# A two-layer diffusion block on one core: the second product of the first FFN by Strassen's scheme, and modulations of layer 1 in other stages

## The chip, the core and the metric

The kernel runs on one core of a Trainium2 chip. The core has a matrix engine (TensorE, PE in the profile; its weight loads are PEld), three engines for elementwise work (VectorE is DVE, ScalarE is ACT, GpSimd is POOL), and SP, whose queue issues most DMAs. TensorE reads SBUF and accumulates in PSUM; VectorE and ScalarE read both memories; GpSimd reads SBUF only. The metric is the device time of one execution in microseconds.

## The reference, cut to what matters

Two layers are applied to 256 tokens `x` and 256 context tokens `ctx`, both of width 1024. Each layer modulates the normalized input, mixes tokens, and runs a convolutional FFN of hidden width 2816. In layer 0 both sequences go through all of it; in layer 1 the context goes into the mixer only.

```python
m = (jax.nn.silu(c) @ mod_w[layer] + mod_b[layer])       # six vectors of 1024, mc likewise from c_ctx
sh1, sc1, g1, sh2, sc2, g2 = jnp.split(m, 6, axis=-1)    # called parts 0 to 5 below
def conv_ffn(u, w_up, conv_w, conv_b, w_down):
    a = dwconv3(u @ w_up, conv_w, conv_b)                # 1024 -> 5632, three taps along the tokens
    gate, val = jnp.split(a, 2, axis=-1)
    return (jax.nn.silu(gate) * val) @ w_down            # 2816 -> 1024: the "second product"
x = x + g2 * conv_ffn(modulate(x, norm2_g, sh2, sc2), ...)
xc = xc + g2c * conv_ffn(modulate(xc, norm2_g, sh2c, sc2c), ...)     # layer 0 only
```

All is float32.

## The kernel before, in words

**Products.** Each float32 operand is split into a high part in the fp32r format, made by ScalarE (`split_w`, L185), and the remainder, made by VectorE as a subtraction with both operands in SBUF (L186). One product of two split operands is a triple of matmuls (`mm3`, L191 to L193): high x high, high x low, low x high. Weights come by DMA on SP's queue in "raw" tiles of 1 MB (`load_raw`), two or more of which exist; the split pieces of 1024 columns have four buffers each for high and low.

**First FFN** (`ffn` with layer 0, called in `layer0`). The hidden width is 22 blocks of 128, taken in pairs, in two parts of 12 and 10 blocks. For every block there are a gate and a value product of 8 triples over 512 columns (256 `x` tokens and 256 context tokens) into one PSUM bank each. `conv3` evacuates a bank: one ScalarE instruction (L459) and two VectorE taps that read PSUM (L462, L463). ScalarE applies silu (L519), GpSimd multiplies gate and value (L520), ScalarE and VectorE split the result into `gh` and `gl` (L521, L522). At the end of a part, for each of two column halves and four token tiles of 128, the second product runs over the part's blocks (`gemm_b`); `resid` multiplies the bank with the gate row `G` and adds it to `x`, both on VectorE (L444, L446). In the last part ScalarE sums the squares for the next norm.

**Modulations.** The layer-0 gate of the FFN and all six parts of layer 1 are computed inside this stage, between pairs and column halves, as "fillers" (`fl`). A filler is one call of `mod_vec` for half a part: four loads of 512 KB (two 128-row slices of weights each), and for each of one or two sequences one multiplication (L306) and seven multiply-accumulates (L308) of 128x512 on VectorE, four TensorE transposes (L312), and a reduction (L314) with one or two small instructions behind it. `gate_rows` makes the rows of `G` from the layer-0 gate: GpSimd builds eight diagonal matrices (L333), TensorE multiplies them with ones.

**Layer 1.** `norm_mod` normalizes both sequences; then the GLA stage (`gla_proj`, `gla_chain`, `gla_out`) interleaves projections with chains of small products on all engines; an output projection, and the second FFN (`ffn` with layer 1) on the 256 `x` tokens. `gate_cols` (L344) spreads a gate over the partitions with TensorE; for the second FFN's gate it stands in the written-out order before that FFN.

**Order.** The tile framework gives each engine its list, in an order that it plans with costs of its own; each engine works through its list in order. Inside `manual_schedule` blocks the order of the named engines is the program's. SP's queue is in order too: a load that waits for its buffer holds up the loads behind it.

Of the kernel before, what the change touches and what calls it, by code (L numbers as in the profile page):

```python
# [9 lines left out]
F32 = mybir.dt.float32  # L10
# [7 lines left out]
D = 1024  # L18
# [88 lines left out]
class Kern:  # L107
# [52 lines left out]
    def load_raw(self, W, kb0, nkb, c0, n):  # L160

        pool, bufs = self.wp, self.RB
        if self.rawp:
            self.nraw += 1
            if self.nraw % (self.RB + self.rawp[1]) >= self.RB:
                pool, bufs = self.rawp
        raw = pool.tile([128, 2048], F32, tag="raw", bufs=bufs, name="raw")
# [7 lines left out]
    def split_w(self, v, pool=None):  # L175
# [11 lines left out]
        return hv, lv  # L187

# [40 lines left out]
    def setup(self):  # L229
        nc, A, const = self.nc, self.A, self.const  # L230
        ncol = sum(k for _, k in COLS)

# [60 lines left out]
    def mod_vec(self, layer, part, half, seqs):  # L293
# [4 lines left out]
        acc = [self.modp.tile([128, 512], F32, tag="macc", bufs=2, name="macc") for s in seqs]  # L298
        for h in range(4):
            raw = self.modp.tile([128, 2, 512], F32, tag="mraw", bufs=self.MB, name="mraw")  # L300
            nc.sync.dma_start(out=raw, in_=W[h * 256 : h * 256 + 256, c0 : c0 + 512].rearrange("(k p) n -> p k n", p=128))
            for k in range(2):
                for s in seqs:
                    c, w = self.cs[:, 2 * h + k, s : s + 1], raw[:, k, :]
# [52 lines left out]
    def square(self, pool, ss, t, c):  # L357

        sq = pool.tile([128, 512], F32, tag="sq", bufs=2, name="sq")
        act = self.nc.scalar.activation(sq, self.x[:, t, c * 512 : c * 512 + 512], AF.Square, accum_out=ss[:, c : c + 1])  # L360
        self.sq_act = act.ins

    def normed(self, pool, ss, t, inplace=False, act=0):
        nc = self.nc
        s1 = pool.tile([128, 1], F32, tag="s1", bufs=4, name="s1")
        nc.gpsimd.tensor_tensor(s1, ss[:, 0:1], ss[:, 1:2], op=ALU.add)
        r = self.rstd(pool, s1, 1, D, "rs")
# [111 lines left out]
    def ffn(self, pool, gpool, layer, nseq, G, fillers, sss, first=None, behind=(), ahead={}):  # L479
# [9 lines left out]
        for p0, p1 in parts:  # L489
# [37 lines left out]
            for c in range(2):  # L527
                self.gemm_b(gt, list(range(p1 - p0)), tiles, Wd, p0, c * 512, 512, mkres(c),
                            last=2 if (c == 1 and p1 == NHB) else 1)
                if fillers:  # L530
                    fillers.pop(0)()

# [304 lines left out]
    def layer0(self):  # L837
# [134 lines left out]
        with fb:  # L972

            with self.pool("ffn0") as fp, self.pool("ffn0g") as fg:
                self.modp, self.MB = fp, 4
                G = fg.tile([128, 2, D], F32, name="G2")
                self.rawp, self.nraw = (fg, 1), -1
# [5 lines left out]
                fl += [lambda p=p, h=h: self.mod_vec(1, p, h, (0, 1) if p < 2 else (0,)) for p in range(6) for h in range(2)]  # L983
# [3 lines left out]
                self.ffn(fp, fg, 0, 2, G, fl, self.sss, first, s0)  # L987
# [194 lines left out]
    def gla_out(self, pool, hp, att, X, Q, K, S=None, later=False):  # L1182
# [14 lines left out]
        os_ = pool.tile([128, 4, 128], F32, tag="gos", bufs=1, name="gos")  # L1197
# [18 lines left out]
    def layer1(self, g4):  # L1216
        nc, A = self.nc, self.A
        W = A["hg_w_in"][0]
        with ExitStack() as bk:
            bk.enter_context(self.banks("hg", mm=4, ga=2, tp=2))  # L1220
            with self.pool("n3") as np_:
                self.norm_mod(np_, self.sss, (0, 1), 1, 0)
            with self.pool("hg") as hg:
# [47 lines left out]
                with self.pool("gla") as gp:  # L1271
                    pr = self.gla_proj(gp, 0, ((), (), self.anch[0], self.anch[1]))
                    ch = self.gla_chain(gp, *pr)
                    values(0)
                    pr = self.gla_proj(gp, 1)
                    self.gla_out(gp, 0, *ch)
                    ch = self.gla_chain(gp, *pr)
                    pr = self.gla_proj(gp, 2)
                    self.gla_out(gp, 1, *ch)
                    ch2 = self.gla_chain(gp, *pr)  # L1280
                    pr = self.gla_proj(gp, 3)
# [10 lines left out]
                    with self.tc.manual_schedule(engines={mybir.EngineType.PE}):  # L1292

                        part_out(acc, w, [(0, 0), (0, 2), (0, 1), (1, 0), (0, 3), (1, 2)])
                        self.gla_turn(3, o3)
                        part_out(acc, w, [(1, 1), (1, 3)])
                        part_out(acc, w, [(k, j) for k in (2, 3) for j in (0, 2, 1, 3)])
                with self.pool("hgo") as hgo:
# [9 lines left out]
                    with self.tc.manual_schedule(engines={E.PE, E.DVE, E.Activation}):  # L1308
# [26 lines left out]
                        self.gate_cols(G4, 1, 5, (0,))  # L1335
# [17 lines left out]
                        self.gate_cols(G4, 1, 5, (1,))  # L1353
# [67 lines left out]
```

## Time and profile before

| | us |
|---|---|
| median of 3 runs | 1172.29 (1170.65 to 1175.51) |
| profiled execution | 1175.04 |
| its span, first to last instruction | 1173.3 |
| TensorE busy | 1137.6 (97%) |
| VectorE busy | 861.5 (73%) |
| ScalarE busy | 519.7 (44%) |
| GpSimd busy | 276.2 (24%) |

The profile is one execution. An engine is busy while an instruction runs on it. Ends of matmuls are modelled and overlap their neighbours, so the distance from start to start is the better price of one. VectorE's instructions also overlap by a little, so that sums of lengths over a stretch are larger than the busy time of the stretch. Idle time is put down to the event that ended it.

### The profile page before, as it was taken

The page shows a single profiled execution, that of the slowest core. Times are in us where ns is not written, and L with a number is a line of the kernel's source. Part 1 is how long each engine was busy: PE and PEld are TensorE (multiplying, and loading weights), DVE is VectorE, ACT ScalarE, POOL GpSimd, SP SyncE. Part 2 cuts the span into 40 slices and gives each one's busy share as a digit, 9 for nine tenths or more (in the row PEclk, how much of TensorE's full clock was granted, in tenths as well). Part 3 has the DMA queues.
Part 4 walks back from the last instruction along what each step waited for, and adds up shares of the span by engine and source line. Part 5 has one row for each costly group of instructions (what it writes and reads, how often), then busy time and mean ns, then how long its engine had stood idle before and what let it go on. Part 6 is the DMA issues. An engine that isn't in the chain of part 4 may idle for free. (4 is left out here: it accounts for less than half of the span.)

```text
span 1173.3 us, 17955 instructions
## 1 busy us (share of the span) xinstructions
PE 1137.6 (97%) x7094; PEld 928.2 (79%) x7094; DVE 861.5 (73%) x1284; ACT 519.7 (44%) x896; POOL 276.2 (24%) x285
## 2 busy tenths in 40 slices
PE   7999988999999999999999999999999999999997
PEld 3587865445888888888888888888888989999985
DVE  4668897786669997989988447565767766877753
ACT  3554333433245444212444236445465456666542
POOL 3110333341011142100111001535657311111110
PEclk9999999998999999999999999999999999999999
DMA  9543221454135552657764223323223354565550
GB/s 338 189 126 90 81 73 43 148 175 154 64 128 196 181 177 93 207 203 246 257 203 138 90 73 108 108 80 102 73 77 105 109 179 140 183 199 173 171 195 36
DMA packets 118055, 167.57 MB, mean 143 GB/s; under 512 B 4658, under 2 KB 74866, under 8 KB 117908
## 3 DMA queue, kind: packets, MB, share of 16 engines
q1 hardware_dynamic: 117540, 165.38, 42.7%
q8 instruction: 56, 0.92, 0.3%
q10 hardware_dynamic: 432, 1.05, 0.2%
q14 instruction: 27, 0.22, 0.1%
HBM read 165.37 MB, written 1.05 MB: 142 GB/s over the span
## 5 line engine op out<-in xcount | busy, mean ns | idle before, releaser
L186 DVE TENSOR_TENSOR lo<-raw,hi 128x1024 fp32r<-128x1024 f32 (+1 forms) x205 | 262.0, 1282 | 151.0 <-ACT hi L185 146.7
L185 ACT CAST hi<-raw 128x1024 fp32r<-128x1024 f32 (+1 forms) x205 | 213.5, 1047 | 325.0 <-PE mm L192 191.8
L192 PE MATMUL mm<-al,hi 128*128 128x512 f32 (+2 forms) x992 | 340.2, 344 | 1.2 <-DVE al L420 1.0
L191 PE MATMUL mm<-ah,hi 128*128 128x512 f32 (+2 forms) x992 | 339.9, 345 | 1.0 <-DVE ah L419 1.0
L193 PE MATMUL mm<-ah,lo 128*128 128x512 f32 (+2 forms) x992 | 340.1, 344 | 0.0
L192 PEld LDWEIGHTS mm<-al,hi 128*128 128x128 f32 x992 | 188.1, 190 | 23.2 <-DVE al L420 1.5
L191 PEld LDWEIGHTS mm<-ah,hi 128*128 128x128 f32 x992 | 187.5, 190 | 23.8 <-DVE ah L419 1.4
L193 PEld LDWEIGHTS mm<-ah,lo 128*128 128x128 f32 x992 | 188.0, 190 | 22.1 <-issue 0.5
L520 POOL TENSOR_TENSOR y<-y 128x512 f32<-128x512 f32 (+1 forms) x44 | 53.5, 1216 | 377.2 <-DVE y L463 319.4
L308 DVE SCALAR_TENSOR_TENSOR macc<-mraw,cs,macc 128x512 f32<-128x512 f32 x140 | 111.1, 804 | 8.7 <-DMA mraw<-in_mod_w_dram 8.0
L191 PE MATMUL mm<-hi,gh 128*128 128x512 f32 x242 | 94.6, 391 | 0.0
L193 PE MATMUL mm<-hi,gl 128*128 128x512 f32 x242 | 94.3, 390 | 0.0
L192 PE MATMUL mm<-lo,gh 128*128 128x512 f32 x242 | 94.2, 390 | 0.0
L191 PE MATMUL mm<-hi,ah 128*128 128x512 f32 (+1 forms) x192 | 74.7, 389 | 0.3 <-DVE modc L285 0.3
L192 PE MATMUL mm<-lo,ah 128*128 128x512 f32 (+1 forms) x192 | 73.7, 384 | 0.0
L193 PE MATMUL mm<-hi,al 128*128 128x512 f32 (+1 forms) x192 | 73.3, 385 | 0.0
L1159 POOL TENSOR_TENSOR gQ<-gQ,gT 128x256 f32<-128x256 f32 x56 | 54.7, 997 | 47.2 <-PE ga L1129 20.4
L1152 DVE TENSOR_TENSOR gK<-gK,gT 128x512 f32<-128x512 f32 (+1 forms) x56 | 50.6, 948 | 13.6 <-ACT gkc L1105 10.4
L193 PEld LDWEIGHTS mm<-hi,gl 128*128 128x128 f32 x242 | 45.4, 188 | 9.5
L192 PEld LDWEIGHTS mm<-lo,gh 128*128 128x128 f32 x242 | 45.4, 188 | 9.3
L191 PEld LDWEIGHTS mm<-hi,gh 128*128 128x128 f32 x242 | 45.4, 188 | 9.2
L459 ACT ACTIVATE y<-mm,col 128x512 f32<-128x512 f32 (+1 forms) x74 | 50.9, 687 | 2.6 <-DVE gl L522 2.6
(301 smaller groups left out, 1779.4 us busy)
## 6 DMA issues: line engine op xcount, KB each, us to landing
mraw<-in_mod_w_dram SPq DMA_DIRECT2D x96, 512.0 KB, 4.7
raw<-in_ffn_w_up_dram SPq DMA_DIRECT2D x44, 1024.0 KB, 5.6
raw<-in_ffn_w_down_dram SPq DMA_DIRECT2D x20, 1024.0 KB, 5.1
raw<-in_hg_w_in_dram SPq DMA_DIRECT2D x20, 1024.0 KB, 5.0
raw<-in_ab_w_in_dram SPq DMA_DIRECT2D x6, 1024.0 KB, 5.2
raw<-in_ab_w_out_dram SPq DMA_DIRECT2D x4, 1024.0 KB, 5.0
raw<-in_hg_w_out_dram SPq DMA_DIRECT2D x4, 1024.0 KB, 5.0
x<-in_x_dram SPq DMA_DIRECT2D x2, 1024.0 KB, 8.3
```

The source lines that it names most:

```text
L185: nc.scalar.copy(hv, v)
L186: nc.vector.tensor_tensor(lv, v, hv.bitcast(F32), op=ALU.subtract)
L191: mm(ps, lhsT=l[0], rhs=r[0], start=start, stop=False)
L192: mm(ps, lhsT=l[0], rhs=r[1], start=False, stop=False)
L193: return mm(ps, lhsT=l[1], rhs=r[0], start=False, stop=stop)
L308: nc.vector.scalar_tensor_tensor(acc[s], w, c, acc[s], op0=ALU.mult, op1=ALU.add)
L459: nc.scalar.activation(y, ps, AF.Identity, scale=w[1], bias=b)
L520: nc.gpsimd.tensor_tensor(ys[1], ys[0], ys[1], op=ALU.mult)
L1152: nc.vector.tensor_tensor(kv, kv, tv, op=ALU.mult)
L1159: nc.gpsimd.tensor_tensor(qv, qv, tq, op=ALU.mult)
```

## The change

The second product of the first FFN is done by a Strassen scheme. In each part the activations are a 2x2 block matrix: rows are the two sequences (`c` for context, `x`), columns the even and the odd blocks of the hidden width; the weights are the matching 2x2 of even and odd blocks by column halves. Seven products of quarters replace eight; they need sums of activation quarters and of weight quarters, which GpSimd makes in float32 before the split, and sums of products, which VectorE makes from one PSUM and one SBUF operand. The parts are now of 3, 3, 2 and 3 pairs. The residual multiplications and additions move to GpSimd, apart from some in the last part. Of layer 1's modulations, parts 3 and 4 (four calls) move into the GLA stage and part 5 (two calls) with its `gate_cols` into the second FFN; outside the first FFN a call loads eight tiles of 256 KB into four tiles kept from the first FFN. In every call ScalarE does the first multiplication. The context's last residual addition is made in layer 1, after the normalization of `x`.

```diff
     def mod_vec(self, layer, part, half, seqs):
+        own, nk = self.modp, 2 if self.modp else 1
+        if own:
+            acc = [own.tile([128, 512], F32, tag="macc", bufs=2, name="macc") for s in seqs]
+        else:
+            acc = [self.const.tile([128, 512], F32, tag="e4", bufs=1, name="macc")]
+        for h in range(8 // nk):
+            if own:
+                raw = own.tile([128, 2, 512], F32, tag="mraw", bufs=self.MB, name="mraw")
+            else:
+                raw = self.const.tile([128, 512], F32, tag=("e1", "u2")[h // 2 % 2], bufs=2, name="mraw").unsqueeze(1)
...
                     if h == 0 and k == 0:
-                        nc.vector.tensor_scalar(acc[s], w, c, None, op0=ALU.mult)
+                        nc.scalar.mul(acc[s], w, c)
...
+    def ffn_both(self, pool, gpool, G, fillers, sss, first, behind):
+        parts = [(0, 3), (3, 6), (6, 8), (8, 11)]
+        A11, A22, A12, S1, S2, S3, S4 = range(7)
+        gh = gpool.tile([128, 3, 7, 256], F32R, name="gh")
+        gl = gpool.tile([128, 3, 7, 256], F32R, name="gl")
...
+        for pa, pb in parts:
+            m, end = pb - pa, pb == 11
+            for pair in range(pa, pb):
...
+                if last:
+                    r11, r12, r22 = quarter(0, 0, pa, m), quarter(0, 1, pa, m), quarter(1, 1, pa, m)
...                                        # up products as before
+                        if last and b > b0:
+                            X = self.raw_tile()[:, : m * 512].rearrange("p (k n) -> p k n", k=m)
+                            nc.gpsimd.tensor_tensor(X, r22, r12, op=ALU.subtract)
+                            nc.gpsimd.tensor_tensor(r12, r12, r11, op=ALU.subtract)
+                            w11 = split(r11)
+                            nc.gpsimd.tensor_tensor(r11, X, r11, op=ALU.add)
+                            r21 = quarter(1, 0, pa, m)
...                                        # conv3, silu, GpSimd product y as before
+                        if b == b0:
+                            nc.scalar.copy(gh[:, g, A11, :], y[:, 256:])
+                            lower(gl[:, g, A11, :], gh[:, g, A11, :], y[:, 256:])
+                        else:
+                            P(sa[:, :256], x1, x2, op=ALU.add)
+                            P(sa[:, 256:], sa[:, :256], c1, op=ALU.subtract)
+                            both(sa, S1)
+                            both(y, A22)
+                            P(sb[:, :256], c1, x1, op=ALU.subtract)
+                            P(sb[:, 256:], c2, sa[:, 256:], op=ALU.subtract)
+                            both(sb, S3)
+                if fillers:
+                    fillers.pop(0)()
...
+            def add(dst, a, b, s=None, c=0, e=nc.vector if end else nc.gpsimd):
+                for t in range(2):
+                    nc.vector.tensor_tensor(dst[t], a[t], b[t], op=ALU.add)
+                    if s is not None:
+                        xs = self.x[:, 2 * s + t, c * 512 : c * 512 + 512]
+                        e.tensor_tensor(dst[t], dst[t], G[:, s, c * 512 : c * 512 + 512], op=ALU.mult)
+                        e.tensor_tensor(xs, xs, dst[t], op=ALU.add)
...
+            product(p1, A11, w11, alls)
+            for t in range(2):
+                nc.scalar.copy(e1[t], p1[t])
+            p6, w6 = banks(), split(r11)
+            nc.gpsimd.tensor_tensor(r11, r21, r11, op=ALU.subtract)
+            p2, w2 = banks(), split(r21)
+            product(p6, S2, w6, head)
+            product(p2, A12, w2, head)
+            product(p6, S2, w6, tail)
+            product(p2, A12, w2, tail)
+            add(u2, e1, p6)
+            add(e1, e1, p2, 1, 0, nc.gpsimd)
+            with self.tc.manual_schedule(engines={E.PE, E.DVE, E.Activation}) if end else ExitStack():
+                product(p5, S1, split(r12), alls)
+                w7 = split(X)
+                add(v, u2, p5)
+                product(p7, S3, w7, alls)
+                w4 = split(r11)
+                add(e4, v, p7, 0, 1, nc.gpsimd)
+                add(u2, u2, p7)
+                product(p4, A22, w4, alls)
+                w3 = split(r22)
+                add(u2, u2, p4, 0, 0)
+                product(p3, S4, w3, alls)
+            if end:
+                self.early = {t: self.factor(self.const, sss[t]) for t in range(2)}
+                add(v, v, p3)
+                for t in range(2):
+                    nc.vector.tensor_tensor(v[t], v[t], G[:, 1, 512:], op=ALU.mult)
+                self.to_ctx = v
+            else:
+                add(v, v, p3, 1, 1, nc.gpsimd)
...
-                self.modp, self.MB = fp, 4
+                self.modp, self.MB = fp, 2
-                self.rawp, self.nraw = (fg, 1), -1
+                self.rawp, self.nraw = (fg, 3), -1
-                fl += [lambda p=p, h=h: self.mod_vec(1, p, h, (0, 1) if p < 2 else (0,)) for p in range(6) for h in range(2)]
+                fl += [lambda p=p, h=h: self.mod_vec(1, p, h, (0, 1) if p < 2 else (0,)) for p in range(3) for h in range(2)]
-                self.ffn(fp, fg, 0, 2, G, fl, self.sss, first, s0)
+                self.ffn_both(fp, fg, G, fl, self.sss, first, s0)
...                                        # layer 1: four calls of mod() around the GLA steps
+                    mods = [(p, h) for p in (3, 4) for h in range(2)]
+                    def mod():
+                        with self.after(self.anch[1]):
+                            self.mod_vec(1, *mods.pop(0), (0,))
...                                        # second FFN
+                fl = [lambda h=h: self.mod_vec(1, 5, h, (0,)) for h in range(2)]
+                fl += [lambda h=h: self.gate_cols(G4, 1, 5, (h,)) for h in range(2)]
-                self.ffn(fp, fp, 1, 1, G4, [], sss, first, s0, ahead)
+                self.ffn(fp, fp, 1, 1, G4, fl, sss, first, s0, ahead)
```

## Rows read from the trace of the kernel before

**Rows 1.** The page: busy us, share of the span, instructions.
```profile
PE 1137.6 (97%) x7094; PEld 928.2 (79%) x7094; DVE 861.5 (73%) x1284; ACT 519.7 (44%) x896; POOL 276.2 (24%) x285
```

**Rows 2.** Stretches: length, busy us of PE, PEld, DVE, ACT, POOL; clock, DMA.
```profile
362.00:705.00 343.00, 343.00 (x1550) 283.33 (x1549) 285.16 (x396) 121.84 (x161) 50.20 (x36) 1.00 0.51 169
...
705.00:960.00 255.00, 254.46 (x2425) 218.99 (x2424) 171.32 (x209) 135.82 (x264) 115.10 (x119) 1.00 0.32 106
960.00:1120.00 160.00, 157.99 (x1233) 153.34 (x1232) 116.39 (x178) 96.87 (x165) 19.26 (x28) 1.00 0.51 169
```

**Rows 3.** Longest of PE's waits, 338 to 720 us: total us, times, longest.
```profile
PE tp L390 <- ACT hm L395: 0.8, 1, 0.8
```

**Rows 4.** Timeline, 676 to 745 us, PE: start, length, engine, line, operation.
```profile
676.07 0.39 PE L193 MATMUL mm<-hi,gl 128*128 128x512 f32 x1
...
678.79 0.39 PE L193 MATMUL mm<-hi,gl 128*128 128x512 f32 x1
...
681.74 0.60 PE L312 MATMUL sc<-ident,macc 128*128 128x128 f32 x4
...
682.09 0.48 PE L191 MATMUL mm<-hi,gh 128*128 128x512 f32 x1
```

**Rows 5.** Timeline of DVE, 386 to 404 us.
```profile
392.85 0.67 DVE L522 TENSOR_TENSOR gl<-y,gh 128x512 fp32r<-128x512 f32 x1
393.45 1.40 DVE L308 SCALAR_TENSOR_TENSOR macc<-mraw,cs,macc 128x512 f32<-128x512 f32 x2
...
396.10 1.21 DVE L186 TENSOR_TENSOR lo<-raw,hi 128x1024 fp32r<-128x1024 f32 x1
397.24 0.73 DVE L308 SCALAR_TENSOR_TENSOR macc<-mraw,cs,macc 128x512 f32<-128x512 f32 x1
397.90 0.73 DVE L462 SCALAR_TENSOR_TENSOR y<-mm,col,y 128x510 f32<-128x510 f32 x1
```

**Rows 6.** DVE's groups by form, 362 to 705 us: busy us, mean ns; idle before.
```profile
L308 DVE SCALAR_TENSOR_TENSOR macc<-mraw,cs,macc 128x512 f32<-128x512 f32 x132 | 105.6, 808 | 8.7 <-DMA mraw<-in_mod_w_dram 8.0
L186 DVE TENSOR_TENSOR lo<-raw,hi 128x1024 fp32r<-128x1024 f32 x61 | 78.5, 1287 | 33.2 <-ACT hi L185 32.8
...
L522 DVE TENSOR_TENSOR gl<-y,gh 128x512 fp32r<-128x512 f32 x22 | 16.5, 749 | 4.6 <-ACT gh L521 4.5
...
L446 DVE TENSOR_TENSOR x<-x,rtmp 128x512 f32<-128x512 f32 x14 | 9.5, 684 | 0.1
...
L306 DVE TENSOR_SCALAR macc<-mraw,cs 128x512 f32<-128x512 f32 x18 | 9.1, 506 | 0.0
```

**Rows 7.** POOL's groups by form, 362 to 705 us.
```profile
L520 POOL TENSOR_TENSOR y<-y 128x512 f32<-128x512 f32 x22 | 36.5, 1659 | 256.0 <-DVE y L463 221.2 <-ACT y L519 25.0 <-DVE modc L315 9.8
L333 POOL TENSOR_TENSOR gdg<-ident,ghi 128x512 fp32r<-128x512 f32 x4 | 6.0, 1506 | 10.1 <-DVE ghi L352 6.9 <-PE sc L334 3.1
```

**Rows 8.** Timeline of DVE and of POOL, 563 to 578 us.
```profile
564.46 2.31 DVE L186 TENSOR_TENSOR lo<-raw,hi 128x1024 fp32r<-128x1024 f32 x1
...
573.57 3.23 DVE L308 SCALAR_TENSOR_TENSOR macc<-mraw,cs,macc 128x512 f32<-128x512 f32 x3
...
564.05 1.64 POOL L520 TENSOR_TENSOR y<-y 128x512 f32<-128x512 f32 x1 [80.59 <-DVE y L463]
573.82 1.64 POOL L520 TENSOR_TENSOR y<-y 128x512 f32<-128x512 f32 x1 [8.14 <-DVE y L463]
```

**Rows 9.** Single lines of code (the last: tile gh): ns least/median/most.
```profile
L186 DVE TENSOR_TENSOR lo<-raw,hi x61: 1204/1218/2312, 362.3 to 694.4; 128x1024 fp32r<-128x1024 f32 x61
L308 DVE SCALAR_TENSOR_TENSOR macc<-mraw,cs,macc x132: 731/743/1772, 361.7 to 644.2; 128x512 f32<-128x512 f32 x132
L520 POOL TENSOR_TENSOR y<-y x22: 1288/1642/2780, 368.6 to 658.2; 128x512 f32<-128x512 f32 x22
L462 DVE SCALAR_TENSOR_TENSOR y<-mm,col,y x44: 729/739/746, 358.6 to 656.5; 128x510 f32<-128x510 f32 x44
L522 DVE TENSOR_TENSOR gl<-y,gh x44: 405/546/1776, 372.8 to 1111.4; 128x512 fp32r<-128x512 f32 x22, 128x256 fp32r<-128x256 f32 x22
```

More of the change, by code (lines that the diff above doesn't have):

```diff
@@ L160, in load_raw @@
     def load_raw(self, W, kb0, nkb, c0, n):
[L162 to L167, printed above, removed]
+        raw = self.raw_tile()
         v = raw[:, : nkb * n].rearrange("p (k n) -> p k n", k=nkb)
@@ L187, in split_w, with raw_tile @@
         return hv, lv
+    def raw_tile(self):
+        pool, bufs = self.wp, self.RB
+        if self.rawp:
+            self.nraw += 1
+            if self.nraw % (self.RB + self.rawp[1]) >= self.RB:
+                pool, bufs = self.rawp
+        return pool.tile([128, 2048], F32, tag="raw", bufs=bufs, name="raw")
     def mm3(self, ps, l, r, start, stop):
@@ L231, in setup @@
         ncol = sum(k for _, k in COLS)
+        for tag in ("e1", "e1", "u2", "u2", "v", "v", "e4"):
+            const.tile([128, 512], F32, tag=tag, bufs=1 if tag == "e4" else 2, name=tag)
         self.ones = const.tile([128, 128], F32R, name="ones")
@@ L297, in mod_vec @@
         W = self.A["mod_w"][layer]
[L298 to L302, printed above, removed]
+        own, nk = self.modp, 2 if self.modp else 1
[8 more added lines that the diff above has]
+                raw = self.const.tile([128, 512], F32, tag=("e1", "u2")[h // 2 % 2], bufs=2, name="mraw").unsqueeze(1)
+            rows = nk * 128
+            nc.sync.dma_start(out=raw, in_=W[h * rows : h * rows + rows, c0 : c0 + 512].rearrange("(k p) n -> p k n", p=128))
+            for k in range(nk):
                 for s in seqs:
-                    c, w = self.cs[:, 2 * h + k, s : s + 1], raw[:, k, :]
+                    c, w = self.cs[:, nk * h + k, s : s + 1], raw[:, k, :]
                     if h == 0 and k == 0:
-                        nc.vector.tensor_scalar(acc[s], w, c, None, op0=ALU.mult)
+                        nc.scalar.mul(acc[s], w, c)
                     else:
@@ L1221, in layer1 @@
             with self.pool("n3") as np_:
-                self.norm_mod(np_, self.sss, (0, 1), 1, 0)
+                self.norm_mod(np_, self.sss, (0,), 1, 0)
+                normed = self.xn_dve
+                with self.after(self.anch[0]):
+                    for t in (2, 3):
+                        xs = self.x[:, t, 512:]
+                        nc.vector.tensor_tensor(xs, xs, self.to_ctx[t - 2], op=ALU.add)
+                        self.square(np_, self.sss[t], t, 1)
+                self.norm_mod(np_, self.sss, (1,), 1, 0)
             with self.pool("hg") as hg:
@@ L1294, in layer1 @@
                         part_out(acc, w, [(0, 0), (0, 2), (0, 1), (1, 0), (0, 3), (1, 2)])
+                        part_out(acc, w, [(1, 1), (1, 3)])
+                        part_out(acc, w, [(2, j) for j in (0, 2, 1, 3)])
                         self.gla_turn(3, o3)
-                        part_out(acc, w, [(1, 1), (1, 3)])
-                        part_out(acc, w, [(k, j) for k in (2, 3) for j in (0, 2, 1, 3)])
+                        part_out(acc, w, [(3, j) for j in (0, 2, 1, 3)])
                 with self.pool("hgo") as hgo:
@@ L1386, in run @@
         self.anch = {}
+        self.early = {}
         self.ORDER = [("c1", 1, 0, 2), ("c1", 0, 0, 1), ("H", 0), ("hy", 2), ("c1", 0, 1, 1), ("H", 1), ("pv", 0, False), ("hy", 3),
```

111 lines of the change are left out of this document (101 added, 10 removed).

## The prediction

> **What bounds the kernel now.** I read the busy totals first: TensorE is busy 97% of the span, VectorE 73% [rows 1]. Then the stretches. The stage that the change rewrites, the first FFN, fills 362 to 705 us: there TensorE is busy 343.00 of 343 us, VectorE 285.16 (83%), ScalarE 121.84, GpSimd only 50.20; the two later stretches that receive the moved modulations hold VectorE at 171 of 255 us and 116 of 160 us, TensorE again nearly full [rows 2]. TensorE's waits from 338 to 720 us are three, the longest of 0.8 us [rows 3]. So the stage ends when TensorE has gone through its list, and a matmul that is taken away is worth its start-to-start distance, unless another engine fills its 343 us first. VectorE has 58 us to spare. The question is what the change puts there.
>
> **TensorE.** The second product is now 22 k-blocks x 4 token tiles x 2 column halves = 176 triples of matmuls. Seven products of quarters are 7 x 2 tiles x 11 k-blocks = 154 triples, of the same shape (128 weights columns, 512 moving). That removes 22 x 3 = 66 matmuls. From 676.07 to 678.79 us twelve such matmuls start, 0.227 us each [rows 4]; the busy time of one is longer because neighbours overlap. 66 x 0.227 = 15.0 us. Six modulation calls (parts 3, 4, 5) also leave the stage; each has four transposes, which push the next matmul back from 681.74 to 682.09 us [rows 4], so 6 x 0.35 = 2.1 us leave here and come back later. TensorE's floor in this stretch falls from 343 to 326 us.
>
> **VectorE, by its own work.** Its instructions start closer together than they last: 0.60 us for a 128x512 subtraction, 0.66 for a scalar_tensor_tensor, 1.14 for a 128x1024 subtraction [rows 5]. The edits at these distances:
> - Modulations: seven accumulating instructions for each call and sequence. 140 fall to 98: -42 x 0.66 = -27.7. The 20 first products go to ScalarE: 0.51 us long [rows 6], about 0.42 apart, -8.4. Six reductions less with their small followers: about -4.
> - Low parts of weights: 22 of 1024 columns (25.1 us) become, for each part of three pairs, 7 x (1.14 + 0.60) = 12.2, three times, and 8.0 for the part of two pairs: 44.5. +19.4.
> - Low parts of activations: 22 x 0.60 = 13.2 become, per pair, three of 512 columns and one of 256 (0.405 us long at least [rows 9], so about 0.34 apart), 11 x 2.14 = 23.5. +10.3.
> - Sums of products: 14 per part, 56 x 0.60 = +33.6.
> - Residual: 16 multiplications and 16 additions leave VectorE, -32 x 0.60 = -19.2; six come back in the last part, +3.6.
>
> Sum +8 us: 285 becomes 293 of 326 us. By this alone VectorE still fits, and the gain of TensorE would stand.
>
> **GpSimd, and what it does to VectorE.** In units of one 128x512 operation, GpSimd has 30 in this stage now: 22 gate-by-value products and 8 diagonal matrices for the gate rows [rows 7]. The change adds four combinations of weight quarters, 4 x 11 = 44 units; four sums of 256 columns per pair, 22; and the residual, 16 units in each of the first three parts and 8 in the last, 56. That makes 152 units.
>
> These are not free for VectorE. From 564.05 us GpSimd runs one product for 1.64 us; a subtraction that VectorE issues at 564.46 lasts 2.31 us in place of 1.22. From 573.82 the next one runs, and three accumulations last 3.23 us together; alone they would have taken 2 x 0.66 + 0.74 = 2.06 [rows 5, 8]. The same shows in the spread: the subtractions of 1024 columns have median 1.218 and maximum 2.312 us, the accumulations 0.743 and 1.772, the GpSimd product 1.288 at least and 2.780 at most, while the convolution taps, which read PSUM, stay between 0.729 and 0.746 [rows 9]. So a VectorE instruction with both operands in SBUF and a GpSimd operation hold each other up; one that reads PSUM is not touched.
>
> Price per unit: mean less median, times count, is (0.808 - 0.743) x 132 = 8.6, (1.287 - 1.218) x 61 = 4.2, and (0.749 - 0.68) x 22 = 1.5 us [rows 6, 9]; 0.68 is the undisturbed length of a 128x512 subtraction [rows 5, 6]. 14.3 us over 30 units is 0.48 us each. The bounds are far apart: zero, if every unit falls under a PSUM-reading instruction or an idle VectorE, and 1.1 to 1.2, what the two collisions of [rows 8] cost when VectorE had SBUF work queued. I take 0.48: it is a mean over the same instructions, at a VectorE load of 83%. About a third of VectorE's time afterwards is PSUM-reading work (88 taps x 0.66 + 56 sums x 0.60 = 92 us of 293), not very different from now, but long combinations of 1536 columns hide worse than short ones and a fuller VectorE hides less. So the value errs on the low side rather than the high one.
>
> 152 x 0.48 = 73 us, against 14.3 now: +59. VectorE 293 + 59 = 352 us, more than TensorE's 326. VectorE becomes the bound of the stage, in-order, with the weight splits that TensorE needs standing behind modulations and sums; the four buffers of split pieces are the slack between the two. With 3% idle left in VectorE the stage takes 352 / 0.97 = 363 us in place of 343: +20 us. ScalarE gets some 42 us more (casts, copies, first products at about the lengths of now) and stays near 164 of 363. What GpSimd itself has, 152 x 1.29 = 196 us plus waits, fits.
>
> In sentences of their own: the Trainium skill, page "SBUF — State Buffer", section "SBUF: two separate sides", calls this port pair an exclusive lock that the first comer keeps for its whole instruction, for a VectorE instruction with two SBUF inputs against a GpSimd one. The collisions above agree in kind; in size, VectorE lost 1.1 to 1.2 us to a product that shows 1.64, so the rows show a shorter hold than the shown span.
>
> **What is moved.** Four modulation calls go into the GLA stage: each 7 x 0.66 + 0.7 = 5.3 us of VectorE, 0.35 us of TensorE, and eight loads of 256 KB on SP's queue, into four tiles, so that the fifth waits for VectorE and the weight loads queued behind it wait too. VectorE has 84 us free there [rows 2] but works in a chain with GpSimd (115 us); between the 1.4 us of TensorE and the whole 21 us I take +3, near the low end because VectorE is 67% busy. Two calls go into the second FFN (10.6 us of VectorE, 44 us free, 4 MB of loads): between 0 and 8, I take +1. The gate columns only change place. At the transition the first sequence's sum of squares is ready before the last product: between 0 and 4 us gained, I take 1. Together +3.
>
> **Sum.** The profiled execution took 1175.04 us, span 1173.3: 1175 + 20 + 3 = 1198. The median of the runs is 1172.29, 2.7 us lower, so the forecast in its terms is **1195 us**.
>
> **Rivals.**
> - *The collisions hide (faster).* The taps, the sums and idle VectorE leave about 92 + 30 us in which GpSimd holds nobody up. If the units are issued mostly there, so that each costs under about 0.28 us (293 - 14 + 152 x 0.28 = 322), TensorE stays the bound: 1172 - 17 + 3 = 1158. For it: some GpSimd products took their least length, 1.288 us [rows 9], beside a VectorE that is busy 83%, and the modulations are filler that can move. Against it: demand is five times as large. Chance 0.26.
> - *GpSimd is late at the four part ends (no change).* Three combinations stand ahead of the last product in its in-order queue, 3 x 3 x 1.29 = 11.6 us; the last activations then miss TensorE's cover (18 + 24 matmuls, 9.5 us) by some 4 us, four times 16 us, which eats the 17. 1172 - 17 + 16 + 3 = 1174. For it: the cover is thin. Against it: the combinations can run during the last pair. Chance 0.12.
> - *The hold is full (much slower).* If no GpSimd operation ever runs beside a two-SBUF VectorE instruction, their times add: 98 x 0.743 + 72 x 1.218 + (21 + 33 + 6) x 0.68 + 11 x 0.41 = 206 us on VectorE, 152 x 1.288 = 196 on GpSimd, 402 us for a stage of 343 (some 5 us lie before it): 397. 1172 + 54 + 3 = 1229. For it: every collision in [rows 8]. Against it: lengths overlap by 0.08 us even without collisions. Chance 0.15. This is what the Trainium skill's page "SBUF — State Buffer", section "SBUF: two separate sides", makes of the time.
> - *The forecast*, 1183 to 1215, has the remaining 0.47.
>
> **How the numbers follow.** What a measurement of this kernel can tell from no change is about 0.5%, 6 us. Faster is the first rival, 0.26; same is the second, 0.12; slower is forecast and full hold, 0.62. The range reaches from the first rival's time to just past the last one's, 1158 to 1230; beyond it lie slack in the schedule better than computed, or PE waits at part ends on top of the hold.
>
> **What would show it.** Right: in the FFN stretch VectorE above 95% busy, GpSimd above 190 us, the mean of the 1024-column subtraction well above 1.29 us, TensorE waiting for VectorE's low parts for tens of us, and the stretch some 20 us longer. Wrong: TensorE still without gaps there and 66 matmuls fewer, the stretch near 326 us. If TensorE's gaps sit only at four places and end on GpSimd, the second rival holds. If VectorE has idle time while the stage is longer, the price per unit was not the step that decides. Gaps in the GLA stage that end on modulation loads would show +3 to be too small.

## The result, and the profile after

The changed kernel takes 1254.72 us (median of four runs, 1253.42 to 1256.51), the kernel before 1171.91 (four runs beside it): ratio 1.0702, 95% interval 1.0675 to 1.0729. Slower, as forecast, but by 83 us and not by 23; the time lies outside the range of 1158 to 1230.

Four marks in TensorE's timeline split the profiled executions (spans 1252.9 and 1173.3). The first is the last but one matmul ahead of a pause in the first product, which both show (2.36 us from it to the first matmul behind the pause): it starts at 345.65 us before, at 341.30 after. The second is the last but one matmul of the second product, the third the first of the last four transposes of the GLA output (tile `gos`), the fourth the last matmul; all are counted from start to start. What lies ahead of the first mark is the same code; its length differs by up to 5 us from execution to execution, so the lengths below are counted from this mark.

| stretch | before | after | difference | forecast |
|---|---|---|---|---|
| first mark to the end of the second product | 363.3 | 420.0 | +56.7 | +20 |
| from there to the last transposes of the GLA output | 239.3 | 262.6 | +23.3 | +2 |
| from there to the last matmul | 216.2 | 220.3 | +4.1 | +1 |

So two thirds of the loss are in the stage that was rewritten ("the stage" from here on is the first line). The page's first line answers to [rows 1]: TensorE has 66 matmuls less and is busy 92% in place of 97% (its busy time is longer all the same, since some of its matmuls ran at a lower clock, see below).

```profile
PE 1154.2 (92%) x7028; PEld 930.0 (74%) x7028; DVE 984.6 (79%) x1345; ACT 565.6 (45%) x973; POOL 484.1 (39%) x401
```

The stretches of the changed kernel, columns as in [rows 2]:

```profile
362.00:705.00 343.00, 293.70 (x1222) 232.22 (x1221) 316.81 (x342) 130.64 (x180) 205.53 (x122) 0.94 0.37 119
...
341.30:660.00 318.70, 268.55 (x1166) 213.69 (x1165) 303.89 (x334) 127.41 (x178) 175.26 (x103) 0.94 0.42 137
660.00:761.28 101.28, 99.99 (x434) 80.82 (x433) 75.75 (x83) 45.41 (x65) 76.00 (x44) 1.00 0.22 72
341.30:761.28 419.98, 368.54 (x1598) 294.51 (x1597) 379.64 (x416) 172.82 (x242) 251.26 (x146) 0.95 0.38 121
```

Read the second line against the third. Up to 660 us VectorE is busy 304 of 319 us (95%) and TensorE has holes. In the last part of the scheme, from 660 us, TensorE is full and VectorE busy 75%. One average over the stage, which the prediction used, hides that. The kernel before has the same unevenness:

```profile
362.00:630.00 268.00, 268.00 (x1214) 221.26 (x1213) 244.91 (x343) 98.19 (x126) 43.58 (x27) 1.00 0.59 193
630.00:705.00 75.00, 75.00 (x338) 62.06 (x337) 40.25 (x54) 23.65 (x35) 6.62 (x9) 1.00 0.25 84
```

Of VectorE's 58 us to spare, 35 stood in the last 75 us, behind the last modulations.

TensorE's longest waits from 340 to 775 us (engine, line, waited for: us in total, times, longest), where [rows 3] had 0.8:

```profile
PE sc L327 <- DVE macc L323: 16.6, 4, 7.6
PE mm L195 <- DVE lo L180: 11.7, 7, 4.5
PE mm L194 <- DVE y L481: 9.9, 2, 5.3
PE mm L194 <- DVE u L668: 5.5, 4, 2.5
```

All four end on VectorE, either at the ends of the parts or at the transposes of a modulation; waits for ScalarE's high parts of the activations come to 4.0 us. VectorE's groups from 362 to 762 us, which answer to [rows 6], are longer throughout; the sums that read PSUM are not:

```profile
L323 DVE SCALAR_TENSOR_TENSOR macc<-mraw,cs,macc 128x512 f32<-128x512 f32 x91 | 105.7, 1173 | 1.0 <-DMA mraw<-in_mod_w_dram 1.0
L180 DVE TENSOR_TENSOR lo<-raw,hi 128x1024 fp32r<-128x1024 f32 x64 | 98.5, 1539 | 19.8 <-ACT hi L179 19.8
...
L668 DVE TENSOR_TENSOR u<-u,mm 128x512 f32<-128x512 f32 x15 | 10.0, 675 | 0.0
```

One part end in the timeline, 400 to 409 us (start, length, engine, line):

```profile
400.93 0.74 DVE L480 SCALAR_TENSOR_TENSOR y<-mm,col,y 128x510 f32<-128x510 f32 x1
401.59 3.48 DVE L323 SCALAR_TENSOR_TENSOR macc<-mraw,cs,macc 128x512 f32<-128x512 f32 x1
...
406.31 0.74 DVE L481 SCALAR_TENSOR_TENSOR y<-mm,col,y 128x510 f32<-128x510 f32 x1
...
401.09 3.43 POOL L617 TENSOR_TENSOR raw<-raw 128x1536 f32<-128x1536 f32 x1 [5.09 <-DVE lo L180]
...
401.53 0.39 PE L196 MATMUL mm<-hi,gl 128*128 128x512 f32 x1
407.20 0.77 PE L194 MATMUL mm<-hi,gh 128*128 128x512 f32 x1 [5.28 <-DVE y L481]
407.76 0.63 PE L195 MATMUL mm<-lo,gh 128*128 128x512 f32 x1
408.19 0.63 PE L196 MATMUL mm<-hi,gl 128*128 128x512 f32 x1
```

GpSimd starts a combination of weight quarters at 401.09. An accumulation that VectorE issues at 401.59, usually 0.74 us, lasts 3.48, until 0.55 us after GpSimd's shown end. The convolution taps behind it, which give TensorE its PSUM bank, come late, and TensorE stands for 5.3 us. Then its matmuls start 0.43 us apart in place of 0.227: the granted clock has fallen from 2.4 to 1.2 GHz (0.50 of full speed from 408 to 412 us). Summed over the start distances of the stage, against those of before, TensorE loses 61.0 us in gaps over 0.15 us, 4.2 in smaller ones and 9.2 at the lower clock, and saves 15.0 with 66 matmuls and some 3 with transposes: +56.6, where the marks give +56.7.

The Trainium skill, page "SBUF — State Buffer", section "SBUF: two separate sides", says that the first comer blocks the other engine for its whole instruction. This row agrees: of GpSimd's 3.43 us, 2.93 were left when the accumulation was issued, and it lasted 2.74 longer than usual.

### The profile page after: what moved, and what is told of

It is laid out like the page before. It is cut to its first block, busy times and chain, and to the rows that moved or that the text cites. A ratio compares the mean times of both kernels' runs of the same rounds, so it can differ in the third digit from the quotient of the medians.

```text
span 1252.9 us, 18215 instructions
## 1 busy us (share of the span) xinstructions
PE 1154.2 (92%) x7028; PEld 930.0 (74%) x7028; DVE 984.6 (79%) x1345; ACT 565.6 (45%) x973; POOL 484.1 (39%) x401
## 3 DMA queue, kind: packets, MB, share of 16 engines
q10 hardware_dynamic: 432, 1.05, 0.2%
HBM read 165.37 MB, written 1.05 MB: 133 GB/s over the span
## 5 line engine op out<-in xcount | busy, mean ns | idle before, releaser
L180 DVE TENSOR_TENSOR lo<-raw,hi 128x1024 fp32r<-128x1024 f32 (+2 forms) x232 | 304.9, 1321 | 107.4 <-ACT hi L179 102.9
L194 PE MATMUL mm<-ah,hi 128*128 128x512 f32 (+2 forms) x992 | 344.2, 349 | 4.2 <-DVE u L668 2.5
L179 ACT CAST hi<-raw 128x1024 fp32r<-128x1024 f32 (+2 forms) x232 | 231.2, 1007 | 253.1 <-PE mm L195 137.0
L323 DVE SCALAR_TENSOR_TENSOR macc<-mraw,cs,macc 128x512 f32<-128x512 f32 x140 | 145.0, 1047 | 5.1 <-DMA mraw<-in_mod_w_dram 4.4
L194 PE MATMUL mm<-hi,gh 128*128 128x512 f32 x220 | 89.7, 418 | 18.2 <-DVE y L481 9.9
L195 PE MATMUL mm<-lo,gh 128*128 128x512 f32 x220 | 89.7, 414 | 11.7 <-DVE lo L180 11.7
L196 PE MATMUL mm<-hi,gl 128*128 128x512 f32 x220 | 86.3, 406 | 0.0
L626 POOL TENSOR_TENSOR y<-y 128x512 f32<-128x512 f32 x22 | 38.7, 1758 | 95.8 <-DVE y L481 59.7
L538 POOL TENSOR_TENSOR y<-y 128x256 f32<-128x256 f32 x22 | 18.1, 821 | 126.4 <-DVE y L481 98.1
```

The lines of the kernel that those rows point to most:

```text
L179: nc.scalar.copy(hv, v)
L180: nc.vector.tensor_tensor(lv, v, hv.bitcast(F32), op=ALU.subtract)
L194: mm(ps, lhsT=l[0], rhs=r[0], start=start, stop=False)
L195: mm(ps, lhsT=l[0], rhs=r[1], start=False, stop=False)
L196: return mm(ps, lhsT=l[1], rhs=r[0], start=False, stop=stop)
L538: nc.gpsimd.tensor_tensor(ys[1], ys[0], ys[1], op=ALU.mult)
```

## The experiments

Theory A: GpSimd's work stretches VectorE's SBUF instructions, and TensorE then waits for VectorE wherever VectorE has no room. Its rivals are in the expectations.

**Are the collisions the cause?** First the changed kernel with GpSimd's new operations cut to 16 columns (combinations, sums and residual are then not computed; the fourth quarter stands in for X):

```
- P(sa[:, :256], x1, x2, op=ALU.add)
+ P(sa[:, :16], x1[:, :16], x2[:, :16], op=ALU.add)
  (the same for the other sums, combinations and residual)
```

> The changed kernel with GpSimd's new operations in the first FFN (combinations of weight quarters, sums of activation quarters, residual products and sums) cut to 16 columns each; the rest of those sums is left out of the computation, a fourth quarter is loaded in place of the first combination. VectorE's and TensorE's lists keep their work. Theory A (the collisions of GpSimd with VectorE instructions that have two SBUF operands fill VectorE): the excess over undisturbed lengths, about 91 us in the stage now, falls to under 20 us, VectorE's busy time from 369 to about 295 us, and the stage (362 us to the last matmul of the second product, now 400 us) to 340 to 350 us; total near 1195 us. Theory B (VectorE's own new work and the planned order cost the time, GpSimd does not): the stage stays within 10 us of 400, total above 1240 us.

1193.92 us, ratio 1.0193 (1.0172 to 1.0214). The stage is 2.9 us shorter than before (342 us in the terms of the expectation, which counts from 362 us): all instructions are still there, GpSimd's are short, and of the 57 us none is left. From 362 to 705 us, columns as above:

```profile
362.00:705.00 343.00, 334.55 (x1474) 269.48 (x1473) 290.92 (x399) 158.77 (x226) 108.64 (x149) 1.00 0.44 140
```

VectorE's own 291 us (I had reckoned 293) cost nothing on balance; some 15 us of gaps more than before remain, mostly at part ends, and use up most of what TensorE saves (15.0 and some 3). Then VectorE's load cut instead (the 70 accumulations of layer 1 in this stage are not computed):

```
-                    else:
+                    elif not own or layer == 0:
                         nc.vector.scalar_tensor_tensor(acc[s], w, c, acc[s], ...)
```

> The changed kernel with the 70 accumulations of layer 1's modulations left out in the first FFN (loads, ScalarE's first products, transposes and reductions stay); GpSimd's work is untouched. Theory A (VectorE's total load, collisions included, is the bound): VectorE loses 70 x (0.66 + 0.43) = 76 us, falls to about 293 us, TensorE becomes the bound again and the stage goes from 400 to 340 to 355 us. Theory C (the chains at the four part ends through GpSimd are the loss, load is not): only the waits for the modulation transposes, about 17 us, go; the stage is near 383 us and the waits of about 40 us at part ends stay.

1209.95 us, ratio 1.0335 (1.0313 to 1.0358). The stage is 10.9 us longer than before. GpSimd's work is whole (234.75 us busy from 362 to 705), so giving VectorE some 80 us of room (70 x 1.17) takes away 46 of the 57. In the expectation's terms the stage is 357 us, 2 above theory A's upper end and far from the rival's 383. The accumulations of the layer-0 gate, 28 of them up to 412.7 us, are still in this run, and VectorE has no more room there than in the changed kernel:

```profile
344.41:410.00 65.59, 59.77 (x320) 50.87 (x318) 63.09 (x74) 32.97 (x47) 27.16 (x15) 0.99 0.48 157
```

TensorE's stop of 5.3 us at the first part end is there again; behind it, where the accumulations are gone, none of its waits is longer than 2.2 us.

**Is it the transposes that stand in TensorE's queue too early?** Each call's transposes and the rest of its end were issued one step later:

```
+ if own and layer == 1:
+     self.mod_late = lambda: self.mod_end(layer, part, half, seqs, acc)
+ else:
+     self.mod_end(layer, part, half, seqs, acc)
```

> The changed kernel with the transposes and reductions of each layer-1 modulation of the first FFN issued one filler later; nothing else is changed. Theory A (VectorE is the bound, TensorE's waits behind the transposes only show its lag): the 17 us of those waits turn into waits for low parts elsewhere, total within 6 us of the changed kernel. Theory D (TensorE's in-order queue behind the transposes is a loss of its own): 12 to 20 us less.

1257.21 us, ratio 1.0737 (1.0719 to 1.0755): nothing gained, as theory A had it. A wait that names a transpose is only where VectorE's lateness shows.

**What does GpSimd's work cost by itself?** The kernel before, with products on a tile that nobody reads:

```
  nc.gpsimd.tensor_tensor(ys[1], ys[0], ys[1], op=ALU.mult)
+ for z in range(6):                                # 3 for half the dose
+     nc.gpsimd.tensor_tensor(idle, idle, idle, op=ALU.mult)   # 448 columns
```

> The kernel before, plus 132 GpSimd multiplications of 448 columns (six behind each gate-by-value product of the first FFN, 116 units of 512 columns) on a tile that nothing reads or waits for. No dependence is added, so only the collisions can cost. Theory A at 0.48 to 0.6 us a unit: VectorE's busy time in 362 to 705 us rises from 285 by 56 to 70 us, to the stage's length; the total rises by 5 to 25 us. Theory C (latency at the part ends, no load): within 3 us of the kernel before.

1228.45 us, ratio 1.05 (1.048 to 1.052): +58 (the stage alone +53), more than twice what I expected at most. Half the dose:

> The kernel before with half the dose of idle GpSimd work: 66 products of 448 columns, 58 units. At 0.47 us each VectorE gets 27 us. The prediction's way of reckoning (whole stage: 285 + 27 = 312 of 343 us, still under 97%): no change, 1168 to 1174. By stretches (from 362 to 630 us VectorE is already busy 245 of 268 us, and 45 units fall there, +21, so it becomes the bound in this stretch although not in the whole stage): +5 to +15, 1176 to 1186. Linear in the dose (half of the +58 of the full one): 1196 to 1203.

1197.98 us, ratio 1.0223 (1.0187 to 1.0259): +25, near the linear rival. Both expectations of theory A missed, and the traces say why. The products depend on nothing, so they ran as early as they could: in the full dose all by 600 us, in the half all by 493. The full dose, then the half:

```profile
345.00:600.00 255.00, 218.75 (x965) 177.16 (x963) 242.31 (x266) 74.06 (x95) 198.65 (x148) 0.94 0.45 144
600.00:758.00 158.00, 158.00 (x710) 130.72 (x709) 115.51 (x156) 57.66 (x80) 19.71 (x17) 1.00 0.49 156
```

```profile
345.00:493.00 148.00, 133.93 (x609) 109.14 (x609) 136.17 (x156) 56.44 (x76) 108.87 (x81) 0.95 0.43 142
493.00:730.00 237.00, 236.90 (x1073) 195.75 (x1071) 189.64 (x267) 75.24 (x100) 23.04 (x21) 1.00 0.53 172
```

While GpSimd works, TensorE has holes; from the moment it stops, none. So the price was paid where the collisions fell, although VectorE had room for all of it later. This was the point to test: the same 36 products (31 units) tied by one column to the gates of the second to fourth pair, or of the last three.

```
+ if layer == 0 and 15 < b:        # early: 1 < b < 8
+     nc.gpsimd.tensor_tensor(idle[:, :1], ys[1][:, :1], ys[1][:, :1], op=ALU.subtract)
+     for z in range(6):
+         nc.gpsimd.tensor_tensor(idle, idle, idle, op=ALU.mult)
```

> The kernel before with 36 idle GpSimd products of 448 columns (31 units) tied to the gates of the last three pairs of the first FFN, where VectorE was busy 48 of 60 and then 18 of 45 us. At 0.47 us each: 15 us for VectorE, less than its room. Room theory: 1170 to 1175. Rival (a collision delays TensorE wherever it falls, 0.43 us a unit as in the run with half the dose): +13, 1183 to 1188.

> The same 36 products tied to the gates of the second, third and fourth pair, about 365 to 460 us, where VectorE was busy 59 of 62 and then 38 of 45 us. Room theory: some 10 us of room for 15 us, +5 to +13, 1176 to 1185. Rival (the whole stage's mean load of 83% decides): 1170 to 1175.

Late: 1171.76 us, ratio 1.0008 (0.9998 to 1.0018). Early: 1181.94, ratio 1.0097 (1.0078 to 1.0116), +11 us. Both are what the theory of room forecast: the same work costs nothing in one place and 11 us in another. Late, the stage and its last 109 us, where the products run; then the same two stretches of the kernel before:

```profile
341.74:705.00 363.26, 362.42 (x1689) 301.59 (x1687) 314.28 (x422) 133.93 (x179) 100.91 (x79) 1.00 0.53 173
596.00:705.00 109.00, 109.00 (x490) 90.16 (x488) 81.67 (x92) 37.47 (x55) 60.41 (x55) 1.00 0.33 106
```

```profile
345.65:708.97 363.32, 362.48 (x1688) 301.50 (x1687) 302.40 (x422) 134.04 (x179) 50.84 (x37) 1.00 0.52 173
600.00:708.97 108.97, 108.97 (x489) 90.16 (x488) 69.13 (x92) 37.64 (x55) 11.50 (x13) 1.00 0.33 107
```

Early, from 407 us:

```profile
407.00:452.00 45.00, 38.34 (x160) 30.11 (x159) 41.20 (x49) 16.15 (x24) 40.61 (x32) 0.96 0.46 148
```

TensorE's longest stop of the early run is shown as ending on GpSimd, on a diagonal matrix of `gate_rows`, and has to be followed one step further back (DVE, POOL, PE):

```profile
424.74 0.16 DVE L352 CAST ghi<-modc 128x16 fp32r<-128x16 f32 x1
425.05 1.88 POOL L333 TENSOR_TENSOR gdg<-ident,ghi 128x512 fp32r<-128x512 f32 x1 [0.78 <-DVE ghi L352]
426.99 0.50 PE L334 MATMUL sc<-gdg,ones 128*128 128x512 f32 x1 [3.76 <-POOL gdg L333]
```

GpSimd had waited for VectorE's cast, and VectorE, without a pause from 404 us on, came to it 9 us later than in the kernel before (counted from the first marks). Three more stops, 1.7 us together, end on diagonal matrices that stood behind the added products in GpSimd's own queue; that part of the 11 us is not VectorE's room.

Late, VectorE does pay for the collisions (314.28 us in place of 302.40 for the same 422 instructions: 11.9 us, 0.38 a unit), and TensorE doesn't notice.

**Can the changed kernel use the room at its end?** Its six modulation calls spread over all pairs:

```
+ m0, m1, m2, m3, m4, m5 = fl[2:]
+ fl = [fl[0], fl[1], m0, none, m1, none, m2, none, m3, none, none, m4, m5, none, none]
```

> The changed kernel with the same six modulation calls in the first FFN, but spread over its pairs up to the last part, in place of one after each of the first eight steps. Theory A (in the changed kernel VectorE is busy 96% up to 660 us and 75% in the 102 us after it, where no modulation stands and TensorE is full, so some 25 us of VectorE's time there are lost to the front): the stage ends 12 to 25 us earlier, total 1230 to 1243. Rival C (the length is set by the part ends, where GpSimd's combinations and the low parts of the weights come late, wherever the modulations stand): within 6 us of 1254.7.

1251.50 us, ratio 1.0671 (1.0642 to 1.07), 3 us less, as rival C had it. The order in the source is not the order on the engines: the last transposes of a modulation moved from 622 to 648 us only. Issuing the last ones behind a later instruction (`with self.after(hold)`) did not move them into the last part either:

> As the run before with spread modulations, but the last two of the six modulation calls are held back until the activations of the ninth and tenth pair are done, so that they really run in the last part, where VectorE was busy 55 of 80 us and TensorE full (in the run before, all of them had still run before 648 us). Theory A (room of VectorE in the last part is lost to the front): the stage ends 8 to 20 us earlier, total 1233 to 1246. Rival C (the part ends set the length, wherever the modulations stand): within 6 us of 1251.5.

1255.31 us, ratio 1.0703 (1.0671 to 1.0735); one accumulation was left behind 660 us. This says nothing on theory A. A true dependence did it:

```
+ if tie is not None:              # one column of that pair's low part
+     nc.scalar.copy(acc[s][:, :1], tie)
  nc.scalar.mul(acc[s], w, c)
```

> Spread modulations again; since issuing later did not move them in the run with held calls (all but the last of their accumulations had still run before 662 us), the last three of the six calls now read one column of the low part of the seventh, eighth and ninth pair's activations counted from zero, so that they cannot start earlier. Theory A (VectorE has room in the last part, 55 of 80 us, that the front cannot use): the stage ends 6 to 15 us earlier than in the changed kernel, total 1238 to 1249. Rival C (the part ends set the length, wherever the modulations stand): 1249 to 1260.

1251.12 us, ratio 1.0684 (1.0668 to 1.07). The stage is 4.9 us shorter than in the changed kernel, and the total gains 3.6: a miss for theory A's size, and inside rival C's range. From the first mark to 660 us, and from there to the second:

```profile
340.82:660.00 319.18, 283.35 (x1234) 226.79 (x1233) 297.77 (x319) 132.40 (x184) 197.77 (x116) 0.94 0.41 130
660.00:755.92 95.92, 86.96 (x367) 69.29 (x365) 89.29 (x98) 40.80 (x62) 51.49 (x31) 0.95 0.32 96
```

Compared with the changed kernel, TensorE idles some 14 us less in front and 8 more behind. The accumulations that went there (19 in 22.31 us, 1.17 each) collide with GpSimd in the last part as they did before; VectorE's total rises by 7 us, to 387 of 415. So the free time in the last part is real, but in this kernel filling it costs more than half of what it gives. All three runs came out where rival C had put them, though only the last one really moved the work. What speaks against it as the whole account is the run without accumulations: GpSimd's combinations stand at the same part ends there, and most of the loss is gone.

**What did the moved calls cost?** The kernel before with the moves alone (with ScalarE's first products and two buffers less for the modulation weights, as in the change), then the changed one without the four calls of the GLA stage (parts 3 and 4 are not computed):

```
- fl += [... for p in range(6) for h in range(2)]
+ fl += [... for p in range(3) for h in range(2)]   # rest as in the change
```

> The kernel before, with the plain second product, and only the move of the six modulation calls of layer 1 (four into the GLA stage, two into the second FFN) made. Prediction's terms: first FFN -2, GLA +3, second FFN +1, total 1170 to 1176. Theory A (the calls themselves cost the GLA stage its extra 16 us, since VectorE and SP's queue have no room there when they are issued): first FFN within 3 us of before, GLA +12 to +18, second FFN +2 to +5, total 1184 to 1192. Rival B (the GLA stage of the changed kernel is longer because of what the new end of the first FFN leaves to it, not because of the calls): GLA within 5 us, total 1168 to 1177.

1193.17 us, ratio 1.0178 (1.0153 to 1.0204): +22. By the marks: -3.1, +13.1, +11.2. The GLA stage is in theory A's range and far from the prediction's +3; the second FFN is more than twice theory A's most.

```
- self.mod_vec(1, *mods.pop(0), (0,))
+ nc.vector.tensor_copy(self.modc[:, 1, p, c, 0], self.modc[:, 1, 0, c, 0])
```

> The changed kernel without the four modulation calls of the GLA stage: parts 3 and 4 of layer 1 are not computed, small copies of part 0 stand in their place. Theory A (the calls cost 16 us there): 1234 to 1243. Rival B (other reasons): within 5 us of 1254.7.

1247.37 us, ratio 1.0645 (1.0613 to 1.0678): only 7 us less, between the two theories. So the calls are dear, but in the changed kernel something else holds the GLA stage up too. The last part by the plain product, with the old end and norm:

```
+ plain = pa == 8                  # gemm_b and the old residual
- self.norm_mod(np_, self.sss, (0,), 1, 0)   # and the late sums
+ self.norm_mod(np_, self.sss, (0, 1), 1, 0)
```

> The changed kernel with the plain second product in its last part (three pairs) and the end of the stage and the norm after it as before; the first three parts by Strassen's scheme, the modulations moved as in the changed kernel. TensorE gets 18 matmuls back, +4.1 us. Theory A (the new end of the stage costs the 7 us up to the first projection and some 5 us of the GLA stage's first half): total 1240 to 1250. Rival B (these come from the moved calls or the order of the GLA stage itself): 1253 to 1262.

1249.84 us, ratio 1.065 (1.0621 to 1.0679). The stage is 1.9 us longer than in the changed kernel, the stretch to the last gos transpose 7.5 us shorter (255.1), the total 4.9 us less: within theory A's range.

**Is there a version that gains?** The scheme for the middle three pairs alone, the plain product around them:

```
+ parts = [(0, 5), (5, 8), (8, 11)];  plain = pa != 5
```

> Strassen's scheme for three of the eleven pairs alone (the middle part, five pairs before it and three after it by the plain product), all modulations of layer 1 in the first FFN and spread so that none stands in the middle part; first products of the modulations on ScalarE. TensorE loses 18 matmuls, 18 x 0.227 = 4.1 us; VectorE gets some 25 us (17 of its own, less 8 for the first products, and 34 GpSimd units more at 0.48) and is then busy 310 of 339 us; the end of the stage is that of before. Theory A (VectorE's work costs only where it has no room): 1166 to 1172. Rival C (every part end of the scheme costs TensorE 5 to 10 us whatever VectorE's load): 1173 to 1180.

1192.13 us, ratio 1.0169 (1.0141 to 1.0196): a miss. In the middle part's end and around it:

```profile
345.00:543.00 198.00, 197.91 (x943) 165.64 (x944) 177.00 (x243) 84.02 (x113) 39.55 (x24) 1.00 0.56 178
543.00:626.00 83.00, 68.09 (x275) 53.62 (x274) 80.82 (x91) 31.22 (x44) 46.27 (x25) 0.92 0.55 174
626.00:725.00 99.00, 99.00 (x446) 81.93 (x445) 78.51 (x98) 38.73 (x58) 26.56 (x21) 1.00 0.38 126
```

The modulations were run there all the same, VectorE is 97% busy, and 15 us are lost in one place where 4 were to be saved. No version run here beats the kernel before.

## Why the prediction failed where it did

- **TensorE's saving**, 15.0 + 2.1 us: right; with it the sum of gaps and clock closes.
- **VectorE's own work**, 293 us: right; 291 with GpSimd cut short.
- **The price of a unit**, 0.48 us: a little low, the side on which the prediction said it would err. Mean less undisturbed length, times count, gives 89 us over 152 units, 0.59: VectorE's load in the stage rose by 77 us, from 302 to 380, where 67 were forecast.
- **The step that failed: "With 3% idle left in VectorE the stage takes 352 / 0.97 = 363 us".** Counted by the marks, the forecast had VectorE idle 14 us of a stage of 383; it was idle 40 of 420. 10 of the 37 us by which the stage was missed are load, 26 are idle time, and 25 of VectorE's idle time lie behind 660 us, where TensorE was full. VectorE bounds the stage only up to there, and there the 3% was nearly right (5%). Room is a matter of place: the same 36 GpSimd products cost nothing behind 600 us and 11 us ahead of 500, in a stage with a mean load of 83%. Held against 362 to 630 us, where the kernel before had 23 us of room, the forecast would have come out higher; by how much was not reckoned. The prediction's own sign for this came true: VectorE with idle time while the stage is longer, so that the price per unit is not the step that decides. What to do with the free 25 us stays open: moving calls into them gave 5 us of the stage back.
- **The clock**: not in the sum at all; 9 of the 57 us.
- **The full hold** (stage +54) came closest, and the row at 401.59 shows such a hold. But its sum let nothing run beside VectorE's SBUF work and knew no stretch that TensorE bounds, so its size is partly chance.
- **Collisions hide**: refuted. A unit cost 0.59 us and not under 0.28, and TensorE did not stay the bound.
- **GpSimd late**: refuted as the main cause. TensorE's long waits end on VectorE, and with GpSimd's work whole but 70 accumulations gone the loss falls from 57 us to 11. As a smaller part it is not excluded: TensorE's own list would take some 346 us (363.3 less 15.0 and some 3); the run with short GpSimd work is 14 us above that, the run without accumulations 28, with its gaps at the part ends.
- **Transition, -1, and GLA, +3**: +23 together. The new end of the stage accounts for 7.5 (plain end), the four calls for 4 (left out) to 13 (all moves alone). By these, 3 to 12 us of the 23 are not settled.
- **Second FFN, +1**: +4, and +11 with the moves alone. The +4 can come about without the two calls: the run with the full dose of idle work, whose code is that of the kernel before from the GLA stage on, has a last stretch of 220.1 us in place of 216.2, and the clock falls there (below). How much of the +11 is the two calls themselves was not tried.

## What to carry to other kernels

Before work is added to an engine that isn't the bound, take its room stretch by stretch, between the points that its work can really move across, not over a stage: the same 36 GpSimd operations cost 0 or 11 us by where they fell. A GpSimd operation on SBUF is VectorE work too, at some 0.4 to 0.6 us per 128x512 here, so moving a sum that takes VectorE 0.60 us itself saves little. And a matmul saved is worth 0.227 us only while nothing makes TensorE stop: a stop costs its length and can be followed by time at half the clock.

## What the runs showed of the hardware

TensorE's long stops in the changed kernel were followed by the lower clock: the 5.3 us at 401.9 by 0.43 us between matmuls in place of 0.227. The length of a stop did not settle it. At the start of the second FFN the kernel before and the run with the full dose of idle work have the same code and the same longest waits (0.8 us for a high part, 0.4 for a low part), and the clock stays in the first and falls in the second (20 us from the same point of each, before and then with the full dose; length, PE busy, count, granted clock, DMA):

```profile
968.28:978.28 10.00, 8.22 (x67) 1.00 0.00 0
978.28:988.28 10.00, 9.77 (x85) 1.00 0.82 265
```

```profile
1017.28:1027.28 10.00, 8.42 (x45) 0.68 0.00 0
1027.28:1037.28 10.00, 10.00 (x74) 0.81 0.65 203
```

What decided between them is not shown. After the wait of 3.5 us for gos (`PE tp L1408 <- DVE gos L1398`) and one of 1.7 us for the high part of the activations (L437), the second FFN of the changed kernel begins so:

```profile
1035.00:1045.00 10.00, 7.92 (x43) 0.97 0.00 0
1045.00:1055.00 10.00, 9.87 (x47) 0.50 0.12 32
1055.00:1065.00 10.00, 10.00 (x65) 0.67 0.96 326
1065.00:1075.00 10.00, 10.00 (x87) 1.00 0.30 98
```

At a granted clock of 0.50 a stretch of 10 us holds 47 matmul records, at 1.00 it holds 87; TensorE is shown busy all the while, so its busy share does not tell of the loss.
